# Replaying the program with the finer timing model when the instruction order is chosen

## The chip, the core and the metric

The kernel runs on one core of a Trainium2 chip. Five engines work on their own lists of instructions: TensorE (PE, with its weight loads shown as PEld), VectorE (DVE), ScalarE (ACT), GpSimd (POOL) and SyncE (SP), which only issues transfers. An engine takes its list from the front; where it has to wait for another engine or for a transfer, what stands behind waits too. The metric is the time of one execution on the device, in microseconds (us), as the median over several executions. The profile shows one further execution with its own time.

## The reference

One encoder layer is applied to two sequences, a long one of 1024 tokens (the "sample") and a short one of 512 (the "prompt"), with the same weights, and a final RMS norm follows. Everything is fp32; the model width is 2048.

```python
h = rms_norm(x, norm_g)
c_val, c_glu, c_gate, q, k, v, a_gate = split(h @ w_in)       # widths 1024 x4, 256, 256, 1024
conv_out = conformer_conv(c_val, c_glu, ...) * silu(c_gate)   # 31 taps along time, layer norm, silu, @ w_pw
attn_out = banded_sink_attention(rope(q), rope(k), v, sink) * silu(a_gate)  # 8 heads, 2 kv heads, window 128
x = rms_norm(x + concat(conv_out, attn_out) @ w_out, final_norm_g)
```

The matrix products dominate: `w_in` (2048 x 5632), `w_pw` (1024 x 1024) and `w_out` (2048 x 2048) for 1536 tokens.

## The kernel before

**Products.** Every fp32 factor is split into a high and a low part (`parts`, L510 on ScalarE and L511 on VectorE), and a product is made of three matmuls: high times high, high times low, low times high. The long sequence's projections go in *units*. A unit takes two blocks of 128 output columns and 1024 rows of a weight, and by sums and differences of blocks gets the eight block products out of seven, named P1 to P7. Each of the seven is 12 matmuls of 512 columns (L207). They accumulate in three PSUM banks, a, b and c, and a bank is shared: P1, P6, P7 and P4 go into bank a one after the other, without clearing it, P2 into b, P5 and P3 into c. After each product the running sum in its bank is read out (`tap`): in the first stages by ScalarE as a copy (L236) and by VectorE as an add (L257), in the output projection by VectorE alone (`Onto.tap`, L304). The next product that goes into the same bank comes one product later. The short sequence's input projection and the pointwise layer run as plain jobs (L670), and the short sequence's output projection comes last (`last_run`, L1852 and, for its last product, L1806).

**Stages in order of time.** The input projection of the long sequence (four stages of units, up to about 850 us), the jobs of the short sequence (to about 1350 us), the pointwise layer of the long one, the output projection of the long one (about 1540 to 1870 us), the pointwise layer of the short one, and its output projection with the final norm.

**Work beside the products.** Weight tiles are loaded by SyncE (L123 and L127 in units, L404 in jobs) into three raw buffers, combined by VectorE (L143) and split into three buffers `hl`. Partial results go to DRAM and come back through GpSimd's queue (L268, L285, L501); `store` (L504) issues most other stores from SyncE's list. Three *lanes* hold the fillers: `conv` (the 31 taps of each of eight channels, L1004 for the short and L1033 and L1041 for the long sequence, on VectorE), `attn` (attention, L1169 to L1211) and `prep` (sums, norms, layer norm, L1465 to L1492; `column_sums` at L701). `tick` hands each lane an allowance in ns after every three matmuls, and the lane's generators then trace their next instructions. So the source writes all engines' work in one interleaved order.

**What sets the order.** That written order is a priority, not yet the order on the engines. On leaving the `TileContext` block a list scheduler takes the whole program, replays it on a simulated core, and on each engine issues next, of the instructions that are ready by that replay, the one of highest priority. Four things bind it: data dependences; buffers (an instruction that needs one waits until the replay has it free); `high_priority(n)`, which moves instructions up by n places (`URGENT` 400 for read-outs and, after the start, weight splits, `SOON` 800 for parts of attention); and `issue_after`, which fixes that an instruction stands behind another on the same engine. `behind` uses the last for the lanes: what a lane traces in a step stands behind the last VectorE and ScalarE instruction traced before that step (`mark`, called by `turn_over`). The orders so found are written into the program, and the semaphores that the chip waits for are placed after that; on the chip nothing is reordered.

The context is opened in `kernel`, at L2173:

```python
    with tile.TileContext(nc) as tc, ExitStack() as ctx:
        encoder(ctx, tc, a)
```

## Time and profile before

| what | value |
|---|---|
| time, median of 3 runs | 2077.31 us (2074.26 to 2078.45) |
| the profiled execution's own time | 2079.13 us |
| its span, first to last instruction | 2077.4 us |
| granted TensorE clock, mean | 0.998 |
| instructions | 27223 |
| busy: TensorE, weight loads | 2060.1 us, 1697.9 us |
| busy: VectorE, ScalarE, GpSimd | 1728.4 us, 1081.8 us, 157.9 us |
| DRAM traffic | 331.77 MB read, 160.96 MB written, 237 GB/s |

Busy time is the time that an engine's instructions cover; waiting, issuing transfers and semaphores don't count. In a row such as `u<-a 128x512 f32<-128x512 f32 x82 | 48.8, 595 | 77.3 <-PE a L207 70.6` stand the output and input by the program's names, partitions by elements, the number of instructions, their busy time in us, the mean length of one in ns, the idle time of the engine just before them, and what ended most of it. A row of the waits has the waiting engine and line, what it waited for, and then the total in us, the number of waits and the longest one. A row of a stretch has its limits and length in us, then for PE, PEld, DVE, ACT and POOL the busy time and number of instructions, the granted clock, the share of the DMA engines and GB/s. "SPq" is SyncE's queue.

### The profile page before, as it was taken

The page shows a single profiled execution, that of the slowest core. Times are in us where ns is not written, and L with a number is a line of the kernel's source. Part 1 is how long each engine was busy: PE and PEld are TensorE (multiplying, and loading weights), DVE is VectorE, ACT ScalarE, POOL GpSimd, SP SyncE. Part 2 cuts the span into 40 slices and gives each one's busy share as a digit, 9 for nine tenths or more (in the row PEclk, how much of TensorE's full clock was granted, in tenths as well). Part 3 has the DMA queues.
Part 4 walks back from the last instruction along what each step waited for, and adds up shares of the span by engine and source line. Part 5 has one row for each costly group of instructions (what it writes and reads, how often), then busy time and mean ns, then how long its engine had stood idle before and what let it go on. Part 6 is the DMA issues. An engine that isn't in the chain of part 4 may idle for free.

```text
span 2077.4 us, 27223 instructions
## 1 busy us (share of the span) xinstructions
PE 2060.1 (99%) x9256; PEld 1697.9 (82%) x9256; DVE 1728.4 (83%) x2843; ACT 1081.8 (52%) x1771; POOL 157.9 (8%) x240
## 2 busy tenths in 40 slices
PE   9999999999999999999999999999999999999998
PEld 8888888888888888788888888888888887888886
DVE  8768899998899899889766777776799978998877
ACT  7486445333465555655555777336553343454454
POOL 0111111111112111100000000000000111100000
PEclk9999999999999999999999999999999999999999
DMA  8888886864577777954555555997789898778897
GB/s 285 309 300 256 200 215 226 286 218 158 190 243 197 181 167 179 279 167 158 164 183 185 178 172 188 316 329 233 239 295 295 279 324 283 213 259 277 293 324 279
DMA packets 242300, 494.56 MB, mean 238 GB/s; under 512 B 23664, under 2 KB 84464, under 8 KB 242160
## 3 DMA queue, kind: packets, MB, share of 16 engines
q1 hardware_dynamic: 216352, 428.83, 62.1%
q0 software_dynamic: 24512, 61.88, 12.5%
q10 hardware_dynamic: 1296, 2.11, 0.3%
q8 instruction: 72, 1.18, 0.2%
q14 instruction: 68, 0.56, 0.1%
HBM read 331.77 MB, written 160.96 MB: 237 GB/s over the span
## 4 chain that ended last, share of the span: by engine, by line
PE 73%; issue 8%; DMA 8%; DVE 7%; ACT 2%; POOL 1%; SPq 0%; ACTq 0%; POOLq 0%; DVEq 0%
PE a L207 21%; PE a L670 13%; PE c L207 10%; PE b L670 6%; PE c L670 6%; PE b L207 5%; PE s L1169 2%; PE pv L1198 2%; PE a L1852 2%; PE s L207 2%; DVE hl L511 2%; PE pt L1203 1%; PE s L1852 1%; DVE t L511 1%; DMA p<-y_d 1%
## 5 line engine op out<-in xcount | busy, mean ns | idle before, releaser
L207 PE MATMUL a<-t,hl 128*128 128x512 f32 x2640 | 632.5, 390 | 1.8 <-ACT u L236 1.3
L207 PEld LDWEIGHTS a<-t,hl 128*128 128x128 f32 x2640 | 493.5, 188 | 108.4 <-ACT u L236 2.4
L511 DVE TENSOR_TENSOR hl<-raw,hl 128x1024 fp32r<-128x1024 f32 (+3 forms) x334 | 337.8, 1012 | 151.5 <-ACT hl L510 147.3
L510 ACT ACTIVATE hl<-raw 128x1024 fp32r<-128x1024 f32 (+3 forms) x334 | 296.8, 889 | 314.4 <-PE c L207 88.1
L670 PE MATMUL a<-t,hl 128*128 128x512 f32 x1344 | 326.3, 393 | 0.0
L207 PE MATMUL c<-t,hl 128*128 128x512 f32 x1320 | 319.1, 389 | 0.0
L670 PEld LDWEIGHTS a<-t,hl 128*128 128x128 f32 x1344 | 248.8, 188 | 50.4
L207 PEld LDWEIGHTS c<-t,hl 128*128 128x128 f32 x1320 | 247.4, 188 | 51.5 <-DVE u L304 0.2
L1041 DVE SCALAR_TENSOR_TENSOR f<-f,c_w_dw,f 128x512 f32<-128x512 f32 x248 | 172.9, 744 | 0.2
L670 PE MATMUL b<-t,hl 128*128 128x512 f32 x672 | 162.9, 392 | 1.5 <-DVE t L515 0.8
L670 PE MATMUL c<-t,hl 128*128 128x512 f32 x672 | 163.9, 393 | 0.0
L1004 DVE SCALAR_TENSOR_TENSOR f<-f,c_w_dw,f 128x512 f32<-128x512 f32 x232 | 163.4, 742 | 0.2
L207 PE MATMUL b<-t,hl 128*128 128x512 f32 x660 | 159.8, 389 | 0.0
L670 PEld LDWEIGHTS b<-t,hl 128*128 128x128 f32 x672 | 124.8, 188 | 27.5 <-DVE t L515 1.1
L670 PEld LDWEIGHTS c<-t,hl 128*128 128x128 f32 x672 | 124.6, 188 | 24.8
L207 PEld LDWEIGHTS b<-t,hl 128*128 128x128 f32 x660 | 123.7, 188 | 25.6
L1033 DVE SCALAR_TENSOR_TENSOR f<-f,w_both,f 128x512 f32<-128x512 f32 x120 | 89.8, 748 | 2.0
L236 ACT ACTIVATE u<-a 128x512 f32<-128x512 f32 x82 | 48.8, 595 | 77.3 <-PE a L207 70.6
L236 ACT ACTIVATE g<-a 128x512 f32<-128x512 f32 x78 | 46.5, 596 | 78.5 <-PE a L207 68.5
L1183 ACT ACTIVATE p<-p,tiny 128x384 f32<-128x384 f32 (+1 forms) x96 | 54.6, 570 | 45.9 <-DVE tiny L1180 36.2
L510 ACT ACTIVATE a<-pt 128x512 fp32r<-128x512 f32 x64 | 38.0, 593 | 64.6 <-PE pt L1203 64.4
L285 POOL DMA_DIRECT2D g<-xT_s x16 | 8.8, 551 | 743.1 <-DMA att_d<-u 669.0
(356 smaller groups left out, 2765.2 us busy)
## 6 DMA issues: line engine op xcount, KB each, us to landing
raw<-w_in SPq DMA_DIRECT2D x170, 512.0 KB, 5.2
raw<-w_out SPq DMA_DIRECT2D x31, 512.0 KB, 5.1
raw<-w_pw SPq DMA_DIRECT2D x24, 512.0 KB, 4.2
wsum_P<-raw SPq DMA_DIRECT2D x47, 256.0 KB, 3.6
raw<-wsum_P SPq DMA_DIRECT2D x18, 512.0 KB, 5.1
f<-x_s SPq DMA_DIRECT2D x16, 512.0 KB, 8.5
g<-wsum_P SPq DMA_DIRECT2D x28, 256.0 KB, 4.6
a<-sum_S SPq DMA_DIRECT2D x24, 256.0 KB, 6.1
```

The costliest lines, as they stand in the source:

```text
L207: nc.tensor.matmul(acc, hl[:, l, o, j, :], toks[j][:, r], start=name in FRESH and j == 0 and q == 0, stop=name in LAST and j == HALF - 1 a ...
L236: nc.scalar.activation(t, bank, AF.Copy)
L510: nc.scalar.activation(hi, x, AF.Copy)
L511: nc.vector.tensor_tensor(lo, x, hi.bitcast(F32), ALU.subtract)
L670: nc.tensor.matmul(job.acc[0], hl[:, l, kk // HALF, kk % HALF, :], r, start=i == 0 and p == 0, stop=i == nk - 1 and p == 2,)
L1004: nc.vector.scalar_tensor_tensor(t, h[:, j : j + T], w(j), t, ALU.mult, ALU.add)
L1033: nc.vector.scalar_tensor_tensor(m0, odd[:, j : j + H], both(j), m0, ALU.mult, ALU.add)
L1041: nc.vector.scalar_tensor_tensor(out, d[:, j : j + H], w(2 * j + k), out if j else m0, ALU.mult, ALU.add)
L1169: nc.tensor.matmul(ps[:, 0:n], qs[:, x, h], k[y][:, keys], start=p == 0, stop=p == 2)
L1183: nc.scalar.activation(p[:, 0:n], p[:, 0:n], AF.Exp, bias=nm[:, h : h + 1], accum_out=l[:, h : h + 1])
L1198: nc.tensor.matmul(pv, v[x][:, vs], pt[:, y], start=i == 0 and p == 0, stop=i == last and p == 2)
L1852: nc.tensor.matmul(acc[t], self.toks[name, m][:, x, i, t * P : (t + 1) * P], parts[i][l].rearrange("p a b -> p (a b)"), start=fresh and fi ...
```

## The change

One argument is added where the context is opened:

```diff
--- before.py
+++ after.py
-    with tile.TileContext(nc) as tc, ExitStack() as ctx:
+    with tile.TileContext(nc, schedule_with_timeline_sim=True) as tc, ExitStack() as ctx:
         encoder(ctx, tc, a)
```

The scheduler then replays the program on another simulated core, whose timing model has more parts (how long an instruction holds its engine and how much later its result lands, queues in front of the engines, the transfer engines), where the plain one has fewer. What is traced, the priorities, the order edges, the buffers and their number are as before. Nothing of the replay is in the program but the order on each engine, the buffers that instructions get, and the semaphores that follow from both.

## The prediction

> **What bounds the kernel now.** I read the engine totals first, then the chain by engine, then busy time in stretches of 50 us, then the waits, then the order of work around a few places.
>
> ```profile
> PE 2060.1 (99%) x9256; PEld 1697.9 (82%) x9256; DVE 1728.4 (83%) x2843; ACT 1081.8 (52%) x1771; POOL 157.9 (8%) x240
> ...
> PE 73%; issue 8%; DMA 8%; DVE 7%; ACT 2%; POOL 1%; SPq 0%; ACTq 0%; POOLq 0%; DVEq 0%
> ```
>
> TensorE is the bound: of a span of 2077.4 us it idles 2077.4 - 2060.1 = 17.3 us. That is the most that any order of the same instructions could give back. Where the 17.3 us lie is in the stretches (columns: PE, PEld, DVE, ACT, POOL busy; granted clock; DMA share; GB/s):
>
> ```profile
> 0.00:50.00 50.00, 48.39 (x207) 40.33 (x208) 42.33 (x69) 34.66 (x58) 1.43 (x6) 1.00 0.86 281
> 50.00:100.00 50.00, 48.91 (x216) 40.16 (x215) 35.62 (x54) 21.50 (x34) 5.97 (x11) 1.00 0.84 306
> ...
> 400.00:450.00 50.00, 50.00 (x222) 41.39 (x221) 48.12 (x73) 17.80 (x27) 5.44 (x10) 1.00 0.78 272
> ...
> 850.00:900.00 50.00, 48.55 (x224) 39.41 (x223) 36.42 (x65) 31.44 (x51) 2.60 (x3) 1.00 0.78 250
> ...
> 1350.00:1400.00 50.00, 48.73 (x220) 40.08 (x219) 34.47 (x54) 16.28 (x22) 0.00 (x0) 1.00 0.94 333
> ...
> 1600.00:1650.00 50.00, 49.47 (x233) 41.44 (x234) 49.69 (x88) 17.90 (x33) 5.48 (x10) 1.00 0.90 288
> ...
> 2050.00:2100.00 50.00, 17.73 (x79) 14.26 (x77) 18.65 (x49) 13.65 (x30) 0.00 (x0) 0.92 0.36 134
> ```
>
> The last stretch holds 27.4 us of the span and 17.73 us of matmuls: 9.7 us of idle time is the tail behind the last matmul. The other 17.3 - 9.7 = 7.6 us lie at the start (1.6 and 1.1 us) and where one stage hands over to the next (1.45 and 1.27 us are the largest). In the middle of a stage a stretch has no idle time and 222 matmuls, 225 ns each. VectorE is close behind there: 48.12 of 50 us in one stretch, 49.69 in another. So the reader is to see one full engine, a second nearly full one that feeds and empties it, and 7.6 us between them that an order can win.
>
> The tail is a chain, one instruction behind the other:
>
> ```profile
> 2056.69 11.04 PE L1806 MATMUL a<-t,t 128*128 128x512 f32 x48
> ...
> 2068.24 0.68 DVE L1729 TENSOR_TENSOR f<-a,f 128x512 f32<-128x512 f32 x1
> ...
> 2072.15 0.58 SPq L1770 DMA_DIRECT2D y_p<-f  x1
> ```
>
> Between the add at 2068.24 and the last store at 2072.15 nothing else waits to be issued, so I let the change have nothing there.
>
> **The change part by part.** It adds and removes no operation by itself: the same 9256 recorded matmuls, 2843 VectorE and 1771 ScalarE instructions and transfers, on the same engines. What it moves is their place in each engine's list. The order written in the source, the priorities and the order edges (a lane's work behind the marks of its step) stay; within them, what is issued next is picked by replaying the program against a timing model, and that model is exchanged. So each term is a question: what happens if instructions that may swap do swap?
>
> *Evictions of a shared bank.* In a unit of seven products the first, P1, leaves bank a, P2 follows in bank b, and P6 then goes on in P1's bank. P1 must have been read out in the time of P2. In the output projection VectorE does that (L304):
>
> ```profile
> 1650.22 3.59 PE L207 MATMUL a<-t,hl 128*128 128x512 f32 x15
> ...
> 1653.64 2.88 PE L207 MATMUL b<-t,hl 128*128 128x512 f32 x12
> 1653.66 0.74 DVE L1004 SCALAR_TENSOR_TENSOR f<-f,c_w_dw,f 128x512 f32<-128x512 f32 x1
> ...
> 1654.33 0.68 DVE L304 TENSOR_TENSOR u<-a,u 128x512 f32<-128x512 f32 x1
> 1654.92 2.06 DVE L1004 SCALAR_TENSOR_TENSOR f<-f,c_w_dw,f 128x512 f32<-128x512 f32 x3
> ...
> 1656.36 2.88 PE L207 MATMUL a<-t,hl 128*128 128x512 f32 x12
> ```
>
> The eviction ends at 1655.01 and the bank is wanted at 1656.36: a margin of 1.35 us. The three taps of the convolution behind it take 2.06 us. Put ahead of it they would stall TensorE 2.06 - 1.35 = 0.7 us; one tap alone (0.74 us) would cost nothing. What queues behind the late eviction is the next matmul and, behind it in TensorE's list, all others. A unit has three such places (P1 to P6, P6 to P7, P7 to P4) and the projection has 16 units: 48 places. The bounds: nothing, if no swap goes that far; 48 x 0.7 = 34 us, if each does. Nothing in the trace says which; I take the middle, 24 x 0.7 = 17 us, because VectorE is nearly full in this stage (49.69 of 50 us above), so that work that can be put ahead is there most of the time, while only a swap by two or more places costs anything. A gain is bounded by the idle time left in the stage, 0.5 us in the stretch above.
>
> In the earlier stages ScalarE evicts (L236, the last two rows); the first row is VectorE waiting for ScalarE's half of a split:
>
> ```profile
> DVE hl L511 <- ACT hl L510: 156.4, 106, 5.6
> ...
> ACT u L236 <- PE a L207: 70.6, 50, 2.1
> ACT g L236 <- PE a L207: 68.5, 50, 2.1
> ```
>
> ScalarE stands ready at 100 of these evictions and waits 139.1 us in all, 1.4 us each; it is 52% busy. I cost this at nothing: the cover is those 1.4 us, and with the cover gone a weight split put ahead costs its own time less 1.4 us, so nothing at 0.9 us (L510 below) and 0.4 us if it is two.
>
> *Splitting the weights.* The two halves of a split:
>
> ```profile
> L511 DVE TENSOR_TENSOR hl<-raw,hl 128x1024 fp32r<-128x1024 f32 (+3 forms) x334 | 337.8, 1012 | 151.5 <-ACT hl L510 147.3
> L510 ACT ACTIVATE hl<-raw 128x1024 fp32r<-128x1024 f32 (+3 forms) x334 | 296.8, 889 | 314.4 <-PE c L207 88.1
> ```
>
> VectorE stands 147.3 us of the 156.4 us above at the head of its list in this one group, for a first half that ScalarE has not made. Another model may put taps there instead. While TensorE never waits for it in mid stage that is worth nothing; three buffers of split weights cover it. With the cover gone each late split costs about 1.0 us (the 1012 ns).
>
> *Transfers.* All loads and most stores share SyncE's list, so a store placed ahead of its data holds the weight loads behind it:
>
> ```profile
> raw<-w_in SPq DMA_DIRECT2D x170, 512.0 KB, 5.2
> ...
> raw<-w_out SPq DMA_DIRECT2D x31, 512.0 KB, 5.1
> ```
>
> A raw tile feeds half a unit, 42 matmuls of 225 ns or 9.5 us, and the load lands 5.2 us after its issue: hidden by 4.3 us; with the cover gone, up to 5.2 us each time. Taken as nothing, with the bad end in the range.
>
> *The taps themselves.* The convolution's taps are the largest filler. What comes of them:
>
> ```profile
> L1041 DVE SCALAR_TENSOR_TENSOR f<-f,c_w_dw,f x248: 723/745/753, 270.1 to 1017.6; 128x512 f32<-128x512 f32 x124
> ...
> L1465 DVE TENSOR_TENSOR t<-t,t x4: 1219/1220/1222, 1112.1 to 1217.7; 128x1024 f32<-128x1024 f32 x4
> ```
>
> The last tap of the long sequence starts at 1017.6 and its result is first used at 1112.1: 94 us of cover, 127 taps of 0.745 us. So a tap's own lateness costs nothing; with the cover gone it is 0.745 us each.
>
> *Table loads.* ScalarE's order decides how often it changes its function table:
>
> ```profile
> L1183 ACT ACT_TABLE_LOAD x13 | 16.7, 1283 | 10.9 <-DVE tiny L1181 10.7
> ```
>
> One more costs 1.28 us of an engine that idles 48%; taken as nothing, against the 1.4 us of cover above.
>
> The sum: 17 us on the profiled execution's own 2079.13 us (span 2077.4 and 1.7 us around it) gives 2096.1 us. That execution lies 1.8 us over the median of 2077.31, so on the median's scale it is 2094 us.
>
> A stall can cost more than its length, by the granted clock (the column before the DMA share):
>
> ```profile
> 1910.85 1.84 PE L701 MATMUL s<-ones,f 128*128 128x1 f32 x16
> ```
>
> ```profile
> 1905.00:1910.00 5.00, 5.00 (x24) 4.14 (x23) 4.13 (x6) 1.80 (x4) 0.00 (x0) 1.00 0.80 251
> 1910.00:1914.00 4.00, 3.94 (x26) 3.34 (x25) 3.02 (x6) 2.40 (x4) 0.00 (x0) 0.99 0.95 327
> 1914.00:1918.00 4.00, 4.00 (x13) 3.10 (x12) 3.69 (x9) 2.36 (x4) 0.00 (x0) 0.58 1.03 374
> ```
>
> After 1.84 us in which TensorE streamed one column at a time the clock fell to 0.58 for 4 us: 13 matmuls where 24 in 5 us make 19 in 4, so 6 x 225 ns = 1.4 us more. Stalls of 0.7 us are shorter than that and take no such addition in my sum; those of 2 us and more do.
>
> The Trainium skill ("TensorE: Matmul & The Clock Gate", "What's actually happening") puts the half clock behind an idle window of about 3.4 us, and advises no idle gaps above about 3 us. By it the sum stays 17 us as well, and only longer gaps than the row's would pay; the row shows a fall after less, with TensorE not even idle by its busy time, so I go by the row.
>
> **The rivals.** *It gives back idle time (not slower).* Place: the 7.6 us outside the tail. Price: all of it, 2079.1 - 7.6 = 2071.5 us, 2070 on the median's scale. It decides from the point where more than 4.2 us of the 7.6 come back, which is 0.2%, about what a measurement of this kernel can tell from no change. For it: VectorE's 147.3 us at the head of its list, which a better order fills with taps, so that they are done before a hand-over. Against it: at the hand-overs it is not VectorE alone that is short.
>
> ```profile
> 1355.00:1360.00 5.00, 5.00 (x24) 4.14 (x23) 1.82 (x2) 1.07 (x1) 0.00 (x0) 1.00 1.01 374
> ...
> 1390.00:1395.00 5.00, 3.73 (x19) 2.74 (x18) 4.60 (x9) 2.86 (x3) 0.00 (x0) 1.00 0.86 268
> ```
>
> Ahead of the 1.27 us stall at 1390 VectorE was busy 1.82 of 5 us and the transfers at 1.01 of their share: no order makes bandwidth.
>
> *Loads fall behind stores (much slower).* Place: SyncE's list. It already stands still for a store whose data is not made:
>
> ```profile
> SPq L504 <- DVE hl L511: 237.7, 47, 11.0
> ```
>
> 47 times, 5.1 us in the mean, 11.0 us at most. A weight load that now stands ahead of such a hold and then stands behind it is late by the hold: 11.0 us less the 4.3 us of cover is a stall of 6.7 us, 8.1 us with the 1.4 us of the clock. It decides where the hold is longer than 4.3 us, and then at 8 of the 47, one in six, it costs 65 us: 2079.1 + 65 = 2144, on the median's scale 2142 us. For it: the models need only disagree on which comes first, a store's data or a free buffer. Against it: a load that could be issued earlier and isn't costs nothing until its cover is used up.
>
> *It does nothing that counts.* Both models may pick the same order, or orders that differ only where the covers above hold: 2077 us. For it: TensorE has no idle time in mid stage, so small swaps are hidden. Against it: a margin of 1.35 us is two taps long.
>
> **How the numbers follow.** Chances: my forecast 0.45, with a range of its own from 2082 (a tenth of the 48 places, 4 us) to 2112 us (all of them); idle time given back 0.20; late loads 0.15; nothing that counts 0.20. The predicted time is the forecast's, 2094 us. The range goes from 2070, all 7.6 us back, to 2142, the late loads as priced; outside lie more late loads than that, several costs at once, and a shorter tail, together less than 2 in 10. Faster: 0.20, the first rival. Within 0.2%: 0.20. Slower: 0.45 + 0.15 = 0.60. The asymmetry is the argument: 7.6 us to win, and margins of 1 to 4 us at hundreds of places to lose.
>
> **What would show it.** Right: TensorE's idle time grows in the stretches from 1500 to 1870 us, waits of TensorE for VectorE at L304 appear, and more taps stand ahead of evictions. The covers: unchanged mid-stage stretches with 222 matmuls before 850 us show that ScalarE's evictions, the splits and the loads stayed hidden; fewer show which did not, by what TensorE or SyncE waits for. Table loads: their count. The clock: further stretches under 1.00. The rivals: less idle time at 850 and 1390 us for the first; weight loads issued later and TensorE waiting for splits of late tiles for the second; equal rows for the third. The forecast is wrong if the stage from 1500 to 1870 us keeps its idle time, or if the tail of 9.7 us changes by more than 2 us.

## The result, and the profile after

The changed kernel takes 2232.09 us (median of 4 runs, 2226.66 to 2235.43) beside 2075.9 us for the kernel before (4 runs): a ratio of 1.0749, with a 95% interval from 1.0723 to 1.0774. The profiled execution took 2231.34 us, its span is 2229.5 us, 152.1 us longer than before. The forecast was 2094 us, with a range to 2142.

The page of the changed kernel, its totals and two of its rows in 40 slices of 55.7 us:

```profile
PE 2115.0 (95%) x9256; PEld 1718.9 (77%) x9256; DVE 1732.6 (78%) x2843; ACT 1076.8 (48%) x1770; POOL 158.0 (7%) x240
...
PE   9999999999999999999999996579998899999997
...
PEclk9999999999999999999999996589999999999999
```

The work is the same, except for one ScalarE instruction (a table load less). TensorE is idle for 114.5 us, where it was 17.3, and is busy for 55 us more with the same matmuls, in good part because the clock was lower for some of them. Both show most at one place, the 25th to 27th slice. The stretches there, and two others:

```profile
1250.00:1300.00 50.00, 50.00 (x230) 41.50 (x229) 31.81 (x53) 28.07 (x43) 0.00 (x0) 1.00 0.51 169
...
1350.00:1400.00 50.00, 25.52 (x70) 15.73 (x70) 28.15 (x53) 28.06 (x56) 0.00 (x0) 0.61 0.42 139
1400.00:1450.00 50.00, 31.64 (x87) 19.44 (x87) 23.32 (x61) 29.09 (x59) 0.00 (x0) 0.57 0.08 29
1450.00:1500.00 50.00, 37.99 (x140) 29.27 (x141) 25.67 (x34) 16.48 (x21) 0.00 (x0) 0.83 0.93 323
...
1650.00:1700.00 50.00, 40.87 (x176) 32.55 (x175) 40.50 (x77) 21.62 (x47) 4.45 (x8) 0.93 0.77 238
```

From 1350 to 1450 us TensorE does 157 matmuls, where a full stretch of 50 us has 230, and in the second half the busy share of the DMA engines falls to 0.08. No engine is full: this is a chain of waits. What runs there, as groups of TensorE's lines from 1360 to 1450 us:

```profile
L1198 PE MATMUL pv<-a,t 128*128 128x512 f32 x36 | 23.2, 720 | 12.8 <-ACT a L510 11.8 <-DVE a L511 1.0
L1203 PE MATMUL pt<-c_ident,p 128*128 128x128 f32 x48 | 15.8, 438 | 20.2 <-ACT p L1190 20.0
L1169 PE MATMUL s<-t,a 128*128 128x384 f32 (+1 forms) x48 | 14.5, 440 | 1.7 <-DVE tiny L1172 1.7
```

It is attention alone; not one matmul of a job (L670) is among them. TensorE works on one attention block after the other, and each step waits for the softmax on ScalarE (L1190) or for the split of the step before (L510).

To see where the 152 us lie I take each stretch less the matmuls in it at the pace that they had in the kernel before (from one start to the next: 227 ns for 512 columns, 176 for 384, 120 for 256, 109 for 128, 112 for one), and call the rest lost. By stage, in us:

```
kernel        0-850  850-1350  1350-1500  1500-1650  1650-1850  later  tail
before          8.7       8.0        2.3        3.6        2.0    2.3   9.6
changed        28.2      22.7       93.8        2.3       29.4    0.8  11.4
```

So 91.5 us of it are the hole, 27.4 the stage of the output projection, 19.5 the units at the start and 14.7 the stretch ahead of the hole. The waits of TensorE agree in kind, with the waits of attention at the top:

```profile
PE pt L1203 <- ACT p L1190: 22.2, 5, 8.4
PE pv L1198 <- ACT a L510: 18.9, 19, 2.9
PE a L207 <- ACT u L236: 6.4, 6, 2.3
...
PE a L207 <- DVE u L304: 2.9, 3, 1.5
```

The hole is made earlier, while TensorE is still full. The first sequence's attention has 16 blocks, and a block is finished by the read-out L1211. In the kernel before, the first eleven come 26.6 us apart (894 to 1160 us), in the changed one 39.7 us apart (931 to 1327 us). So the eleventh comes 167 us later: 36 us by which the first block is late already, and 131 us of slower blocks. When the 1700th job matmul starts, the kernel before has all 16 blocks behind it, the changed one 11. Of the 13 us that a block takes longer, 10.3 lie between its first transpose and its last product (19.7 us against 9.4, the mean of the second to the eleventh block). One step of a block shows why. TensorE and VectorE of the changed kernel, from its timeline:

```profile
1126.79 0.27 PE L1203 MATMUL pt<-c_ident,p 128*128 128x128 f32 x1
1126.82 5.25 PE L670 MATMUL c<-t,hl 128*128 128x512 f32 x22
1131.90 0.40 PE L1198 MATMUL pv<-a,t 128*128 128x512 f32 x1
...
1127.73 0.69 DVE L511 TENSOR_TENSOR a<-pt,a 128x512 fp32r<-128x512 f32 x1 [0.91 <-ACT a L510]
```

And the same step in the kernel before:

```profile
1040.18 0.60 PE L1203 MATMUL pt<-c_ident,p 128*128 128x128 f32 x4
1040.54 2.33 PE L670 MATMUL a<-t,hl 128*128 128x512 f32 x9
1042.70 0.86 PE L1198 MATMUL pv<-a,t 128*128 128x512 f32 x3
...
1041.45 0.69 DVE L511 TENSOR_TENSOR a<-pt,a 128x512 fp32r<-128x512 f32 x1 [5.70 <-ACT a L510]
```

The split is ready 0.56 us ahead of the products before (1041.45 + 0.69 to 1042.70), and 3.48 us ahead of them after: 15 job matmuls stand between. I counted, for the 44 such steps of the first sequence, the job matmuls that start between the end of the split and the start of its products (a negative number: the first product, which needs only the high half, starts ahead of it):

```
before   -5 to -1: 21 steps,  0: 12,  1 to 2: 11
changed          0: 18 steps,  2 to 14: 8,  15: 17,  16: 1
```

With the plain model no step has more than 2; with the finer one 18 of 44 have 15 or 16, and none has more. I call such a step, at which work comes back to an engine that others fill meanwhile, a hand-back. The cap at 16 looks like a queue in front of the replayed TensorE, filled with job matmuls before the product was ready. A replay that reckons each split as done later by a fixed time would give the same counts. The replay itself was not looked into, so which of the two it is stays open; the lateness itself is shown.

### The profile page after: what moved, and what is told of

The parts are those of the page before. It is cut to its first block, busy times and chain, and to the rows that moved or that the text cites. A ratio compares the mean times of both kernels' runs of the same rounds, so it can differ in the third digit from the quotient of the medians.

```text
span 2229.5 us, 27383 instructions
## 1 busy us (share of the span) xinstructions
PE 2115.0 (95%) x9256; PEld 1718.9 (77%) x9256; DVE 1732.6 (78%) x2843; ACT 1076.8 (48%) x1770; POOL 158.0 (7%) x240
## 4 chain that ended last, share of the span: by engine, by line
PE 82%; DVE 6%; DMA 6%; ACT 4%; issue 2%; SPq 0%; ACTq 0%; DVEq 0%
PE a L207 23%; PE a L670 13%; PE c L207 11%; PE c L670 6%; PE b L670 6%; PE b L207 6%; PE pv L1198 2%; PE s L207 2%; PE a L1852 2%; PE s L1852 2%; PE s L1169 2%; DMA raw<-w_in 1%; PE pt L1203 1%; PE pt L207 1%; PE pv L1852 1%
## 5 line engine op out<-in xcount | busy, mean ns | idle before, releaser
L207 PE MATMUL a<-t,hl 128*128 128x512 f32 x2640 | 648.5, 393 | 17.8 <-ACT u L236 6.4
L510 ACT ACTIVATE hl<-raw 128x1024 fp32r<-128x1024 f32 (+3 forms) x334 | 295.5, 890 | 312.4 <-PE a L207 49.7
L670 PE MATMUL a<-t,hl 128*128 128x512 f32 x1344 | 326.0, 394 | 6.8 <-DVE hl L511 5.4
L207 PE MATMUL c<-t,hl 128*128 128x512 f32 x1320 | 325.3, 391 | 4.8 <-ACT g L236 4.0
L670 PEld LDWEIGHTS a<-t,hl 128*128 128x128 f32 x1344 | 250.5, 189 | 60.0 <-DVE hl L511 6.3
L207 PE MATMUL b<-t,hl 128*128 128x512 f32 x660 | 170.4, 390 | 0.0
L670 PE MATMUL c<-t,hl 128*128 128x512 f32 x672 | 164.8, 397 | 3.4 <-DVE g L1070 2.0
L670 PE MATMUL b<-t,hl 128*128 128x512 f32 x672 | 163.4, 397 | 4.5 <-ACT g L936 2.6
L670 PEld LDWEIGHTS b<-t,hl 128*128 128x128 f32 x672 | 126.8, 191 | 32.2 <-ACT g L936 3.3
L670 PEld LDWEIGHTS c<-t,hl 128*128 128x128 f32 x672 | 125.5, 190 | 30.6 <-DVE hl L511 1.8
L236 ACT ACTIVATE u<-a 128x512 f32<-128x512 f32 x82 | 49.0, 597 | 144.9 <-PE a L207 137.7
L236 ACT ACTIVATE g<-a 128x512 f32<-128x512 f32 x78 | 46.6, 597 | 138.2 <-PE a L207 120.0
L511 DVE TENSOR_TENSOR a<-pt,a 128x512 fp32r<-128x512 f32 x64 | 44.1, 689 | 76.4 <-ACT a L510 76.2
L510 ACT ACTIVATE a<-pt 128x512 fp32r<-128x512 f32 x64 | 38.1, 595 | 119.9 <-PE pt L1203 119.4
L1198 PE MATMUL pv<-a,t 128*128 128x512 f32 x132 | 57.8, 502 | 22.4 <-ACT a L510 17.5
```

The costliest lines, as they stand in the source:

```text
L207: nc.tensor.matmul(acc, hl[:, l, o, j, :], toks[j][:, r], start=name in FRESH and j == 0 and q == 0, stop=name in LAST and j == HALF - 1 a ...
L236: nc.scalar.activation(t, bank, AF.Copy)
L510: nc.scalar.activation(hi, x, AF.Copy)
L511: nc.vector.tensor_tensor(lo, x, hi.bitcast(F32), ALU.subtract)
L670: nc.tensor.matmul(job.acc[0], hl[:, l, kk // HALF, kk % HALF, :], r, start=i == 0 and p == 0, stop=i == nk - 1 and p == 2,)
L1198: nc.tensor.matmul(pv, v[x][:, vs], pt[:, y], start=i == 0 and p == 0, stop=i == last and p == 2)
```

## The experiments

Three theories stood at the start. H: hand-backs to TensorE are late, so the attention lane falls five blocks behind the jobs and is made good alone. B: the hole comes of buffers. S: many lists differ a little everywhere. What spoke for B is the moment at which the jobs stop. A product in bank b ends by 1308.6 us, and its read-out (L936) comes in ScalarE's list behind everything of attention that is late:

```profile
1306.03 2.56 PE L670 MATMUL b<-t,hl 128*128 128x512 f32 x10
...
1455.47 1.28 ACT L936 ACT_TABLE_LOAD   x1
1456.77 0.60 ACT L936 ACTIVATE g<-b 128x512 f32<-128x512 f32 x1
```

It writes a tile of the tag `g`, and so do two of the four block sums that attention makes at a time (L1284 to L1287; the other two go to the tag `u`), which are traced earlier and wait for attention. All ratios below are to the kernel before, run beside it on the same chip, with their 95% intervals.

**Block sums in place (changed kernel).**

```diff
-            self.block_sums(1, j, x[0][1], x[1][1])
+            self.sums_in_place(1, j, x[0][1], x[1][1])
```

> The changed kernel, with the block sums of the attention half (four tiles of the read-outs' tag each time) made in place in the tiles of their operands, so that no read-out has to wait for a tile that an earlier block sum holds. B: the hole from 1350 to 1500 us closes and nothing takes its place: 2232 - 92 = 2140 us. H: the lane is still five blocks behind and must be made good before the next stage reads its results; the hole moves to the end of the jobs, near 1440 to 1610 us, and the time stays within 40 us of 2232, more likely above it.

2256.5 us, ratio 1.0863 (1.0845 to 1.0881). The hole went from its place and came back 150 us later, larger:

```profile
1350.00:1400.00 50.00, 50.00 (x230) 41.48 (x229) 33.80 (x58) 33.11 (x54) 0.00 (x0) 1.00 0.70 243
...
1500.00:1550.00 50.00, 21.20 (x68) 13.89 (x67) 29.91 (x59) 24.18 (x43) 0.00 (x0) 0.62 0.70 241
...
1650.00:1700.00 50.00, 29.99 (x87) 18.55 (x86) 14.35 (x46) 20.34 (x51) 0.55 (x1) 0.64 0.20 58
```

Lost are 0.9 us from 1350 to 1500, and 146.6 from 1500 to 1850 (31.7 in the changed kernel). B falls: the buffers only set the place at which the lag is collected. H had the place a little early.

**Fewer hand-backs.** All transposes of a block are traced together, two of the three sets into the score banks, and its products together.

```diff
+        pts = []
         for i in range(hi - lo):
-            tp = e.PS("pt", [GROUP, P])
+            tp = e.PS("s" if i else "pt", [GROUP, P])
...
-            yield S5
-            products(i, pt)
+        for i, pt in enumerate(pts):
+            yield S5
+            products(i, pt)
```

> The changed kernel, with TensorE's order left free, but fewer hand-backs in an attention block: all transposes of the block are traced together (the second and third go to the two score banks), and its products follow together, so that TensorE is asked two times less per block. H: each hand-back saved is worth about 3.4 us of the block's 38 us; at 31 us per block the lag at the 1740th job matmul falls from five blocks to two or three, the loss in 1350 to 1500 us falls from 92 to about 40 us: 2130 to 2180 us, and lower if the lag no longer reaches the buffers. B and S: nothing is changed in the buffers of the read-outs or in the lists of the other engines: within 15 us of 2232.

2142.7 us, ratio 1.0310 (1.0295 to 1.0326): 90 us off the changed kernel. The first eleven blocks come 31.2 us apart, and at the 1700th job matmul 14 are done, not 11. Lost from 1350 to 1500 are 40.3 us, and 7.0 from 1650 to 1850. The control is the same edit in the kernel before:

> The kernel before, plain model, with the same edit as the run with fewer hand-backs (the transposes of an attention block traced together, its products together). It is the control of that run, which took 90 us off the changed kernel. H: in the plain model's lists a hand-back costs nothing that counts, so there is nothing to save: 2065 to 2085 us. If this is faster by 50 us or more, the edit is good by itself and its 90 us say nothing of the finer model.

2076.07 us, ratio 0.9993 (0.9982 to 1.0004): nothing. So the edit is worth 90 us with the finer model's lists, where hand-backs are late, and nothing with the plain model's.

**The lag without the finer model.** The kernel before with `RUSH = 1.2` in place of 1.8.

> The kernel before, plain model, with the attention lane's pace in the job stage cut from 1.8 to 1.2, so that it is traced a third slower and falls behind the jobs without any other change. H: a lane that is behind must be made good alone, whichever model orders it: a stretch of attention alone appears behind the jobs, with a granted clock well under 1, and the time is 2130 to 2200 us. Against it (the lag is only a companion of the loss): within 15 us of 2076.

2187.2 us, ratio 1.0520 (1.0504 to 1.0537). Its blocks come 36.8 us apart. It loses 49.9 us from 1500 to 1650, most of it in one wait for a read-out on VectorE, whose list stands meanwhile at attention's sums (L1305), and 62.7 from 1650 to 1850, where the second sequence's blocks run alone:

```profile
PE a L670 <- DVE g L1533: 40.7, 1, 40.7
...
DVE a L1305 <- DMA a<-ag_d: 27.8, 7, 10.3
```

```profile
1750.00:1800.00 50.00, 30.64 (x83) 18.99 (x83) 13.71 (x43) 20.06 (x51) 1.65 (x3) 0.60 0.13 37
```

That is 110 us over the kernel before, so a late lane is dear with the plain model's lists too.

**TensorE's list as traced.** An order edge from every matmul to the next one in the source, in both kernels; the two TensorE lists are then the same, line by line.

```diff
     last.last_run(at)
+    traced(tc, lambda n: True)
+
+def traced(tc, pick):
+    info = mybir.DependencyInfo(mybir.DependencyClass.NoSync, mybir.DependencyReason.DATA)
+    on = [i for i in tc.nc.cur_bb.bb.instructions if i.engine == mybir.EngineType.PE]
+    for n in range(1, len(on)):
+        if pick(n / len(on)):
+            tc.add_manual_dep(on[n], on[n - 1].name, info, reason="traced")
```

> The changed kernel, with an order edge from every TensorE matmul to the next one traced, so that TensorE's list is the order of the source; the other lists stay free under the finer model. Theory H (hand-backs): the finer model's replay issues job matmuls to TensorE ahead of their execution, so an attention product that has become ready is placed some 3.5 us late, an attention block takes 38 us in place of 26, the lane falls five blocks behind and is made good alone; the 92 us lost from 1350 to 1500 us, the 13 us from 1000 to 1100 and the 27 us from 1650 to 1850 all come of it. With TensorE's list as traced they go: 2232 - 132 = 2100 us, with at most 5 us lost in any of these three stretches. Theory B (buffers): the loss comes of read-outs that wait in ScalarE's list behind block sums, whatever TensorE's order is: ScalarE's list is still free, so the stretch from 1350 to 1500 us still loses 50 us or more, 2180 us or more. Theory S (spread): the other engines' lists lose the time: 2200 us or more.

> The kernel before with the same edges: TensorE's list as traced, the other lists by the plain model. It is the control of the run above. H: the plain order's overtaking is worth little, since the lane's pace in the source is already about right: 2076 to 2110 us. If it is 2150 us or more, the traced order of TensorE is itself a bad one, and the run above cannot tell the theories apart.

With the finer model 2208.9 us, ratio 1.0624 (1.0607 to 1.0640); with the plain one 2111.1 us, 1.0161 (1.0146 to 1.0176). The second is 1 us over its range and does as a control. The hole is closed in the first (7.8 us lost from 1350 to 1500), as H says, but the time is not won: 75.7 us are lost from 850 to 1350, in many short waits for attention's work on ScalarE and VectorE. The waits of the first run, and the same wait in the second:

```profile
PE pt L1203 <- ACT p L1190: 21.6, 30, 4.5
PE pv L1198 <- DVE a L511: 16.8, 11, 4.3
```

```profile
PE pt L1203 <- ACT p L1190: 6.4, 18, 2.0
```

One TensorE list, and 98 us between the two: H, as I had put it (2100 us), missed, and the time is the one that theory S had named (2200 us or more). H is only half of the cause. The other lists of the finer model are late too.

**Lists of before, held one by one.** The program is scheduled twice in the build: with the plain model, to read its lists, and then with the finer one, with order edges that hold the chosen engines to the lists of the plain one.

```diff
+    E = mybir.EngineType
+    lists = program(False, (), None)[1]
+    nc = program(True, (E.PE, E.DVE, ), lists)[0]
...
+            for engine in held:
+                for n, m in zip(lists[engine], lists[engine][1:]):
+                    tc.add_manual_dep(
+                        by_name[names[m]], names[n],
+                        mybir.DependencyInfo(mybir.DependencyClass.NoSync, mybir.DependencyReason.DATA), reason="held",
+                    )
```

> The program is scheduled twice in the build: once with the plain model, to get the list of each engine of the kernel before, and then with the finer model, with order edges that hold TensorE to its list of before; VectorE, ScalarE, SyncE and GpSimd are ordered by the finer model. The run with TensorE as traced (2208.9 us, against 2111.1 us for the same TensorE list beside the plain model's other lists) leaves two theories. L (the other lists): the finer model's lists of the other engines serve TensorE late whatever its list is: 2076 + 98 = about 2174 us, at least 2150. T (the traced list): the traced TensorE list was only unlucky beside them, and the kernel before's own list mends it: 2076 to 2110 us.

> As the run before, with VectorE held to its list of before too; ScalarE, SyncE and GpSimd are ordered by the finer model. D (VectorE): what serves TensorE late is VectorE's list, on which taps are issued ahead of attention's and the splits' instructions, and the loss goes: 2070 to 2095 us. A (ScalarE or the queues): it stays at 2150 us or more.

> The finer model with VectorE alone held to its list of before; TensorE is ordered by the finer model. H (hand-backs on TensorE): an attention product that becomes ready still finds some 17 job matmuls issued ahead of it, and now VectorE, bound to its list, waits for the late lane as well: no better than 2232 us, up to 2300. D alone (VectorE's list is the whole cause): 2080 to 2120 us.

> The finer model with TensorE, VectorE and ScalarE held to their lists of before; only SyncE and GpSimd are ordered by it. With TensorE and VectorE held it was 2112.3 us, 35 over before. ScalarE's list is what is left: 2074 to 2085 us. The transfers' lists are what is left: 2105 us or more.

| engines held to their lists of before | us | ratio (interval) | lost 850-1350 | lost 1350-1500 |
|---|---|---|---|---|
| none (the changed kernel) | 2232.1 | 1.0749 (1.0723 to 1.0774) | 22.7 | 93.8 |
| VectorE | 2289.1 | 1.1015 (1.0998 to 1.1033) | 117.4 | 32.7 |
| TensorE | 2199.0 | 1.0586 (1.0566 to 1.0606) | 66.8 | 6.7 |
| TensorE, VectorE | 2112.3 | 1.0166 (1.0147 to 1.0184) | 31.4 | 2.3 |
| TensorE, VectorE, ScalarE | 2085.6 | 1.0038 (1.0023 to 1.0053) | 8.7 | 0.3 |

L stands, and T falls. Held in this order, VectorE's list is the largest part once TensorE's is right: 87 us; ScalarE's is 27, and what SyncE and GpSimd order is 8. The 2112 us lie between the two ranges expected, over D's 2070 to 2095, by ScalarE's part; the 2085.6 us are 0.6 over theirs. VectorE alone makes it worse by 57 us: it is bound to the order in which a lane on time would come, and waits for the late one, most of all at attention's splits (the first row, beside the changed kernel's):

```profile
DVE a L511 <- ACT a L510: 194.3, 54, 8.1
```

```profile
DVE a L511 <- ACT a L510: 77.1, 37, 6.2
```

What VectorE's list does, with TensorE held (ScalarE's, VectorE's and TensorE's timeline):

```profile
1249.69 0.59 ACT L510 ACTIVATE a<-pt 128x512 fp32r<-128x512 f32 x1
...
1250.89 1.20 DVE L1489 TENSOR_TENSOR t<-t,t 128x1024 f32<-128x1024 f32 x1
1250.91 0.07 DVE L941 MEMSET f<- 128x15 f32 x1
1252.02 2.35 DVE L1489 TENSOR_TENSOR t<-t,t 128x1024 f32<-128x1024 f32 x2
1254.29 0.68 DVE L1006 TENSOR_TENSOR f<-f 128x512 f32<-128x512 f32 x1
1254.89 0.68 DVE L511 TENSOR_TENSOR a<-pt,a 128x512 fp32r<-128x512 f32 x1
...
1255.63 0.74 PE L1198 MATMUL pv<-a,t 128*128 128x512 f32 x2 [3.63 <-DVE a L511]
```

The high half is made at 1250.28. VectorE, after a tap in hand, does three layer-norm instructions of 1.2 us and an add, none of which TensorE waits for, and starts on the low half 4.6 us later; TensorE stands for 3.63 us. It is the hand-back again, to VectorE. That this lateness, summed over the list, is all of the 87 us was not separated further.

**The late TensorE list alone.** The converse: the plain model for all but TensorE, which is held to its list of the changed kernel.

> The converse: the plain model orders VectorE, ScalarE, SyncE and GpSimd, with TensorE held to its list of the changed kernel (the program is scheduled with the finer model first, to get that list). H: the late products stand in TensorE's list itself, so the lane is late and the hole from about 1350 to 1500 us is there without any other list of the finer model: 2170 to 2235 us. If the hole needs the other lists too: under 2130 us.

2261.4 us, ratio 1.0879 (1.0861 to 1.0897), over the upper end expected. Lost from 1350 to 1500 are 90.7 us, and the first eleven blocks come 40.6 us apart. The hole is in TensorE's list, and the plain model cannot mend it with the others. So either half is enough: the finer TensorE list beside plain lists costs 184 us, the plain TensorE list beside finer lists 122, both finer 156. They don't add; I take it that lists which are late together wait for each other less than lists made by different models, but no run shows that by itself.

**The clock in the hole.** 162 matmuls that compute nothing that is used, in the blocks that run in the hole.

```diff
+    def fill(self, g, b, qs, n):
+        if self.s == 0 and g == 1 and b >= 4:
+            t = self.e.PS("s", [GROUP, P])
+            for _ in range(n):
+                self.e.nc.tensor.matmul(t, qs[:, 0, 0], qs[:, 0], start=True, stop=True)
...
+                if h == GROUP - 1:
+                    self.fill(g, b, qs, 24)
...
+            self.fill(g, b, qs, 6)
```

> The changed kernel, with 162 more matmuls of 512 columns (36.8 us at 227 ns) that compute nothing that is used: in the last four attention blocks of the first stream, which run in the hole, 24 behind the scores and 6 behind each set of transposes, into a score bank, where TensorE has to wait anyway. C (clock): in the hole the granted clock is 0.57 to 0.62 because TensorE is not kept busy; with the filling it rises, the blocks (22 us each in the hole) go faster and the time falls by 10 to 30 us in spite of the added work: 2200 to 2222 us. Without it: the added work lies in idle time or lengthens the blocks a little: 2230 to 2250 us.

```profile
1350.00:1400.00 50.00, 37.92 (x147) 27.30 (x146) 23.40 (x59) 30.02 (x63) 0.00 (x0) 0.83 0.49 155
1400.00:1450.00 50.00, 40.00 (x169) 30.87 (x168) 26.30 (x65) 26.31 (x56) 0.00 (x0) 0.86 0.06 16
```

2241.7 us, ratio 1.0789 (1.0770 to 1.0807): not faster than the changed kernel (1.0749), by the medians 9.6 us slower. The clock rose from 0.61 and 0.57 to 0.83 and 0.86, and the last four blocks still take 22.3 us each (1371 to 1460 us), where they took 22.0 (1367 to 1455). So the time did not fall as C had it. But the clock is not without a price: in those four blocks the matmuls of attention took 36.7 us in place of 49.7. TensorE's groups there, in the filled kernel (L1156 are the fillers) and in the changed one:

```profile
L1156 PE MATMUL s<-a 128*128 128x512 f32 x162 | 39.7, 397 | 0.9 <-DVE tiny L1178 0.9
L1206 PE MATMUL pv<-a,t 128*128 128x512 f32 x34 | 15.9, 539 | 15.1 <-ACT a L510 7.6 <-DVE a L511 7.3
L1175 PE MATMUL s<-t,a 128*128 128x384 f32 (+1 forms) x44 | 12.2, 410 | 1.9 <-DVE tiny L1178 1.9
L1211 PE MATMUL pt<-c_ident,p 128*128 128x128 f32 x44 | 8.6, 311 | 0.1
```

```profile
L1198 PE MATMUL pv<-a,t 128*128 128x512 f32 x34 | 21.9, 720 | 14.0 <-ACT a L510 13.2 <-DVE a L511 0.7
L1203 PE MATMUL pt<-c_ident,p 128*128 128x128 f32 x44 | 14.8, 440 | 20.2 <-ACT p L1190 20.0
L1169 PE MATMUL s<-t,a 128*128 128x384 f32 (+1 forms) x44 | 13.0, 431 | 1.7 <-DVE tiny L1172 1.7
```

The fillers stand in the same list ahead of attention's next matmuls and make them late: reckoned from the end of the softmax, the first transposes of the four blocks start 6.6 us later in sum. What the fillers cost in the chain and what the clock saves were not separated further, so the clock's own price stays open.

No version beat the kernel before.

## Why the prediction was wrong, point by point

**The direction was right, the size was not: 2232 us, outside the range.** The step that failed is the frame of the sum: "So each term is a question: what happens if instructions that may swap do swap?" Every term was then a swap priced at the place where it stands, against a cover of its own. Attention was no term at all. But a lane whose blocks are a chain through three engines (scores, softmax, transposes, splits, products) adds up its lateness: 13 us in each block, 39.7 against 26.6, and no cover of a single step shows that. The cover that counted is how far a lane may fall behind the jobs before its results are needed; five blocks was too many.

**The bound.** "One full engine" with at most 7.6 us to win was right, and so was that margins outnumber gains. That TensorE had no idle time in mid stage was read as cover ("small swaps are hidden"). It says only that TensorE's own list is full, not that the lanes inside it have slack.

**Evictions of a shared bank, 17 us.** Mis-sized: 3 waits and 2.9 us (L304 in the waits above), of 48 places. I had said that more idle time from 1500 to 1870 us and waits at L304 would show the forecast right. Both came, with 27.4 us lost from 1650 to 1850; yet TensorE waits there mostly for attention and for splits, and with TensorE and VectorE held the loss is 1.1 us. A sign that fits two causes was no test.

**Evictions by ScalarE, nothing.** Wrong by some 11 us. The units up to 850 us now wait for L236 in 15 places, 13.0 us, where it was 1.6:

```profile
PE a L207 <- ACT u L236: 5.1, 5, 2.3
PE a L207 <- ACT g L236: 4.3, 6, 0.9
PE c L207 <- ACT g L236: 3.6, 4, 1.5
```

In nine of these places (6.2 us) ScalarE is not late: it starts the read-out as soon as the product ends. TensorE's own list has the next product of the same bank right behind it, with none between, so that it waits for the whole read-out:

```profile
703.03 2.88 PE L207 MATMUL a<-t,hl 128*128 128x512 f32 x12
706.60 3.64 PE L207 MATMUL a<-t,hl 128*128 128x512 f32 x14 [0.69 <-ACT g L236]
```

In the other six (6.8 us) ScalarE is still at other work; the longest wait, 2.3 us, comes of a norm (L514) that had itself waited 2.1 us for a transfer. The cover of 1.4 us took it for granted that the product between stays in its place, and that is a swap in TensorE's list which the sum didn't ask about.

**Splits, transfers, taps, table loads, tail.** These held, or nearly: the splits of weights, put at nothing, are 5.4 and 4.2 us in the largest rows of TensorE's waits for them over the whole span, no row of those waits names a load, ScalarE has one table load less in all, and the tail is 11.4 us after 9.6, within the 2 us named.

**The clock.** The fall of the clock was foreseen for stalls of 2 us and more, and it came: 0.57 in the hole. Whether a stall therefore costs more than its length was not settled there: the fillers raised the clock and made attention's matmuls shorter, and the blocks were no shorter. The Trainium skill ("TensorE: Matmul & The Clock Gate", "HAM oscillation — how this bites in real kernels") reckons the penalty of throttled matmuls as half of their time. By it the 57.2 us of busy TensorE from 1350 to 1450 us held at most an estimated 28.6 us to win (the clock there was 0.57 to 0.61); in the run with the fillers attention's matmuls gave up 13.0 us of 49.7, and the time won none of it, in a chain that the fillers delay too.

**The rivals and the range.** Idle time given back: no. Late loads: no. Nothing that counts: no. The range ended at eight late loads, because the worst that I had thought of was a stall repeated; "several costs at once" was put under 2 in 10 without a price. The lower end of the forecast's own range is a slip: a tenth of 48 places at 0.7 us is 3.4 us, not 4, so 2081 and not 2082. And one reading was wrong where it mattered. The row that I took as "Ahead of the 1.27 us stall" lies some 30 us ahead of it; in the five stretches of 5 us from 1365 to 1390 us VectorE was busy for 4.25 to 5.00 us. The stall itself was attention's scores waiting for two splits, a hand-back in the kernel before:

```profile
1391.45 0.50 PE L1169 MATMUL s<-f,a 128*128 128x256 f32 x2 [0.51 <-ACT a L510]
1392.71 0.73 PE L1169 MATMUL s<-f,a 128*128 128x256 f32 x4 [0.76 <-DVE a L511]
```

## What to carry to other kernels

Before changing what orders a program, look for the lanes that are chains through several engines, and ask for each how late it may get before the main stream needs it: a few microseconds at each hand-back are invisible in the totals and add up to one large hole later. Where a hole is found, look for its cause ahead of it, in a stretch where the main engine still looks full: freeing the buffer at which the main stream stopped only moved the hole. And hold one engine's list at a time to the good order; it tells in a few runs which list carries the loss, and that two half-changed sets of lists can be worse than either.

## What the hardware showed that was not expected

In a chain of dependent steps the granted clock sat at 0.57 to 0.61 for 100 us while TensorE was busy for more than half of the time (25.5 and 31.6 of 50 us), and the transposes of a block took 438 ns each where they take 273 among jobs. Filling TensorE to 37.9 and 40.0 us of 50 brought the clock to 0.83 and 0.86, shortened attention's matmuls in the last four blocks from 49.7 to 36.7 us, and left the time of a block at 22 us.
